# The even layer's order of chunks: the Fourier columns (context) and the context's output projection between the latent ranks' products and their use, and a tile of its own for `kvt`

## The chip, the cores and the metric

The kernel runs on one core of one Trainium2 chip. The metric is the device time of one execution in microseconds (us). Five engines work side by side and wait for each other by semaphores: TensorE (PE) does matrix products and transposes, VectorE (DVE), ScalarE (ACT) and GpSimd (POOL) do elementwise work, and SyncE (SP) issues the loads of the weights.

## The reference

Two blocks, one behind the other. The first has two layers (retention, dilated attention, gated MLP, and a feed-forward part). The second has an even and an odd layer, over 256 positions `x` and 256 positions of a context `ctx`. The change lies in the even layer alone:

```python
def mla_kv(kv_a, k_pe, kv_norm, w_kvb, rope):
    kv = (rmsnorm(kv_a, kv_norm) @ w_kvb).reshape(b, n, 8, 64 + 64)    # latent rank 256
    ...
def even_layer(h_lat, h_ctx, w_in, q_norm, w_qb, kv_norm, w_kvb, w_out, rope, ctx_out):
    f_in, f_gate, q_a, kv_a, k_pe, m_gate = split_cols(h_lat @ w_in, EVEN_SPLITS)
    cf_in, cf_gate, cq_a, ckv_a, ck_pe, cm_gate = split_cols(h_ctx @ w_in, EVEN_SPLITS)
    k_c, v_c = mla_kv(ckv_a, ck_pe, kv_norm, w_kvb, None)
    k_l, v_l = mla_kv(kv_a, k_pe, kv_norm, w_kvb, rope)
    q_l = mla_q(q_a, q_norm, w_qb, rope)                               # latent rank 384
    a_l = blocked_dense_attention(q_l, concat(k_c, k_l), concat(v_c, v_l), MLA_SCALE)
    y_l = concat([fourier_mix(f_in) * silu(f_gate), a_l * silu(m_gate)]) @ w_out
    q_c = mla_q(cq_a, q_norm, w_qb, None)
    a_c = dense_attention(q_c, k_c, v_c, MLA_SCALE)
    y_c = concat([fourier_mix(cf_in) * silu(cf_gate), a_c * silu(cm_gate)]) @ w_out
    return y_l, y_c
```

`h_lat` and `h_ctx` are the normed and modulated `x` and `ctx`. `fourier_mix` is the real part of a two-dimensional Fourier transform over positions and group columns.

## The kernel before, in words

Products in full accuracy: every float32 operand is split into a high and a low part, and each product is done as three products of the parts (`mm3`, `mmT`). Weights come from memory in pieces of up to 128x1024 (`raw`, three in flight in this layer), are split by ACT (`whi`) and by DVE or POOL in turn (`wlo`) into a ring of five, and a piece goes back to the ring when its last product is done. `plan` lists the pieces in the order of use, and SP's queue loads them in that order.

The even layer is one generator, `even_pass(b)`, run for `b = 0` (context) and `b = 1` (latents, the 256 positions of `x`). Each `yield` ends a step, and each step is one chunk of products over 256 positions:

- `kv`: 288 columns, the rank of keys and values with the rotary columns. Each tile of 128 positions is normed into `ka`, and a task transposes `ka`, splits it into `kvt` (`to_split`), and does the same for the rotary columns (`kp` into `kpT`).
- `qa`: 384 columns, the queries' rank, normed into `qa`, transposed and split by a task into `qtT`.
- `kvb`: keys `kT` and values `vs` from `kvt`. `qb`: queries `qT`, `qr` from `qtT`. After `qb` two tasks (`heads_task`) do the attention: four units of two heads for the context, eight for the latents, two at a time. The latents' eight are called four rounds here.
- `fi`: 512 columns; a task does the Fourier transform in four groups (`aa`, `yf`). `fg`, `mg`: gates of 512 columns each. `wo`: the output projection, two halves of 512 columns, eight blocks of the contraction each; blocks 0 to 3 need the Fourier part, 4 to 7 the attention.

When the context's `wo` is done, `modnorm_task` norms, transposes and modulates the context again (`crow`) for the odd layer.

TensorE's program is written in order at build time. A small planner (`Flow`) keeps an estimate of the time of each engine; after each `mm3` or `mmT`, `pump` lets up to three tasks whose due time has come write their next matmuls. Where a chunk needs a result (`F.wait`), the planner runs tasks until the result is due. So the tasks' matmuls stand between the products of whatever chunk is being written. The programs of ACT, DVE and POOL are ordered by the scheduler, by priorities; each of those engines takes its instructions in order.

In the kernel before, `kvt` is the tile `junk` (one buffer), which the norm of the latents at the end of the first block (`modnorm_task` with `junk`, events `eev[1]`) uses too. The `kv` tasks of both passes therefore yield until `eev[1]` of both tiles is set (lines 1744 and 1745).

Of the kernel before, what the change touches and what calls it, by code (L numbers as in the profile page):

```python
# [12 lines left out]
F32R = mybir.dt.float32r  # L13
BF16 = mybir.dt.bfloat16
I32 = mybir.dt.int32
AF = mybir.ActivationFunctionType
# [4 lines left out]
P = 128  # L21
# [98 lines left out]
LAT = 0.22  # L120
TR = "tr"
# [204 lines left out]
def block_kernel(ctx: ExitStack, tc: tile.TileContext, A, out, stop=None):  # L326
    nc = tc.nc
    pe = nc.tensor
    F = Flow()
    act, dve, gp = (Lane(F, n, e) for n, e in (("act", nc.scalar), ("dve", nc.vector), ("pool", nc.gpsimd)))  # L330
# [29 lines left out]
    def trtile(dt=F32):  # L360
        F.take_tr()
        return pt.tile([P, 512], dt, name="tr")
# [5 lines left out]
    def mm(o, lhsT, rhs, start, stop_, cost=None, **kw):  # L368
        n = 1
        for s in o.shape[1:]:  # L370
            n *= s
        pe.matmul(o, lhsT, rhs, start=start, stop=stop_, **kw)  # L372
        if cost is None:
            cost = max(0.107, n * 0.417e-3 + 0.003) if lhsT.dtype == F32R else 2 * max(0.107, n * 0.833e-3 + 0.003)
        F.now += cost
        F.chain = max(F.chain, F.now + LAT)
# [138 lines left out]
    def chunk_plan(b, key):  # L515
        if key == "kvb":
            for k in range(2):
                add(("e", b, key), A["e_w_kvb_2"][0], k, 1, [(0, D)])
        elif key == "qb":
            for k in range(3):  # L520
                add(("e", b, key), A["e_w_qb_2"][0], k, 1, [(0, 768)])
        elif key == "wo":
            for h in range(2):
                for k in range(0, 8, 2):
                    add(("e", b, "wo", h), eo, k, 2, [(h * 512, 512)])
        else:
            cc, n = {"kv": (1408, 288), "qa": (1024, 384), "fi": (0, 512), "fg": (512, 512), "mg": (1696, 512)}[key]
            add_chunk(("e", b, key), ew, cc, n, key in ("fg", "mg"))
    E_STEPS = ["kv", "qa", "kvb", "qb", "fi", "fg", "mg", "wo"]
    E_ORDER = [0] * 7 + [1] * 4 + [0] + [1] * 4  # L530
    at_step = [0, 0]
    for b in E_ORDER:
        chunk_plan(b, E_STEPS[at_step[b]])
        at_step[b] += 1
    ow, oo = A["o_w_in_2"][0], A["o_w_out_2"][0]
    for key, cc in (("kv", 1024), ("q0", 0), ("q1", 512), ("g0", 1536), ("g1", 2048)):
# [1041 lines left out]
    def work(name):  # L1578
        return w2.tile([P, 512], F32, name=name, tag="w")
# [11 lines left out]
    def etile(tag, shape, bufs=1, dt=F32, name=None):  # L1591
        return ep.tile([P] + shape, dt, name=name or tag, tag=tag, bufs=bufs)
# [11 lines left out]
    def chunk(key, n, toks, xs, evs, evac):  # L1604

        w = by_k(take(key, 4))
        for i, t in enumerate(toks):
            z = mmtile()
            for k in range(8):
                if k % 4 == 0:  # L1610
                    F.wait(evs[t][k // 4])
                mm3(z[:, :n], xs[t][0][:, k], xs[t][1][:, k], w[k], k == 0, k == 7)
                F.pump()
                if i == len(toks) - 1 and k % 2:
                    done()
            F.from_pe()
            evac(t, z)
# [86 lines left out]
    def even_pass(b):  # L1704
# [12 lines left out]

        def kvt_tile():
            if not box:
                box.append(jp.tile([P, 2, 2, 256], F32R, name="kvt", tag="junk"))  # L1720
            return box[0]

        def evac_kv(t, z):
            sq = small("ss")
            act.activation(dump(256), z[:, :256], AF.Square, scale=1.0 / 16.0, accum_out=sq)
            c = F.chain
            kp = etile("kp", [4, 32], 2)
            src = z[:, 256:288]
            if b == 1:
                kr = etile("kr", [64])  # L1730
                rotate(kr[:, :32].rearrange("p (h d) -> p h d", h=1), src.rearrange("p (h d) -> p h d", h=1),
                       axm[:, t * 64:(t + 1) * 64], 1, 16, kr[:, 32:64], dve)
                src = kr[:, :32]
            act.activation(kp, src[:, None, :].to_broadcast([P, 4, 32]), AF.Copy)
            F.chain, c = c, F.chain
            r = power(sq, "rkv", 1.0, EPS)
            ka = work("ka")
            F.chain = max(c, F.chain)
            act.activation(ka[:, :256], z[:, :256], AF.Copy, scale=r)
            F.free_mm()  # L1740

            def task():
                yield
                yield eev[1][0][1]
                yield eev[1][1][1]
                yield TR
                tr = trtile()
                for j in range(2):
                    transpose(tr[:, j * P:(j + 1) * P], ka[:, j * P:(j + 1) * P], ident)
                tc_ = slice(t * P, (t + 1) * P)  # L1750
                kvt = kvt_tile()
                to_split(tr, [col("e_kv_norm_2", j) for j in range(2)], kvt[:, 0, :, tc_], kvt[:, 1, :, tc_])
                F.free_tr()
                F.set(kv_ev[t])
                yield TR
                tr = trtile()
                transpose(tr[:, :P], kp.rearrange("p a f -> p (a f)"), ident)
                n0 = (2 * b + t) * P
                F.from_pe()
                halves(kpT[:, 0, n0:n0 + P], kpT[:, 1, n0:n0 + P], tr[:, :P])  # L1760
                F.free_tr()
                F.set(kp_ev[t])
            F.spawn(task())
# [39 lines left out]
            F.spawn(task())  # L1803
        chunk(("e", b, "qa"), 384, range(2), xs, evs, evac_qa)
        yield

        n0 = 2 * b * P
        w = by_k(take(("e", b, "kvb"), 2))
# [155 lines left out]
            F.spawn(heads_task(par))  # L1964
        yield

        def evac_fi(t, z):
            us[t] = etile("g2", [512], 4, name="us")
            act.activation(us[t], z, AF.Copy)
            F.free_mm()  # L1970
            F.set(u_ev[t])
        chunk(("e", b, "fi"), 512, range(2), xs, evs, evac_fi)
        yf = etile("yf", [4, 256])

        def fourier_task():
            yield u_ev[0]
            yield u_ev[1]
            for g in range(4):
                yield TR
                tr = trtile()  # L1980
                for a in range(2):
                    mm(tr[:, :258], us[a][:, g * P:(g + 1) * P], dft[:, a * 258:(a + 1) * 258], a == 0, a == 1)
                t3 = tr[:, :258].rearrange("p (s n) -> p s n", s=2)
                aa = work("aa").rearrange("p (s n) -> p s n", s=2)
                act.activation(aa[:, :, 0:128], t3[:, :, 0:128], AF.Copy)
                F.chain -= LAT
                act.activation(aa[:, 0, 128:256], t3[:, 0, 128:0:-1], AF.Copy)
                F.chain -= LAT
                act.activation(aa[:, 1, 128:256], t3[:, 1, 128:0:-1], AF.Copy, scale=-1.0)
                F.free_tr()  # L1990
                yield TR
                tr = trtile()
                mm(tr[:, :256], cds[:, 0:P], aa[:, 0], True, False)
                mm(tr[:, :256], cds[:, P:2 * P], aa[:, 1], False, True)
                act.activation(yf[:, g], tr[:, :256], AF.Copy)
                F.free_tr()
            F.set(yf_ev)
        F.spawn(fourier_task())
        yield

        sgf, sgm = [None, None], [None, None]

# [7 lines left out]
        def product_task():  # L2010
            yield yf_ev
            for i in range(2):
                yield gf_ev[i]
                dst = yf[:, 2 * i:2 * i + 2].rearrange("p k n -> p (k n)")
                gp.tensor_tensor(dst, dst, sgf[i], op=OP.mult)
                F.set(yg_ev[i])
        yg_ev = [Ev(), Ev()]
# [12 lines left out]
        def split_task():  # L2030
            for i in range(2):
                yield yg_ev[i]
                v = yf[:, 2 * i:2 * i + 2]
                act.activation(XH[b][:, 2 * i:2 * i + 2], v, AF.Copy)
                dve.tensor_tensor(XL[b][:, 2 * i:2 * i + 2], v, XH[b][:, 2 * i:2 * i + 2].bitcast(F32), op=OP.subtract)
                for k in (2 * i, 2 * i + 1):
                    F.set(yT_ev[k])
            for i in range(2):
                yield gm_ev[i]
                for h in range(4 * i, 4 * i + 4):  # L2040
                    yield at_ev[h]
                v = at_box[0][:, 2 * i:2 * i + 2]
                vf_ = v.rearrange("p k n -> p (k n)")
                dve.tensor_tensor(vf_, vf_, sgm[i], op=OP.mult)
                k0 = 4 + 2 * i
                act.activation(XH[b][:, k0:k0 + 2], v, AF.Copy)
                dve.tensor_tensor(XL[b][:, k0:k0 + 2], v, XH[b][:, k0:k0 + 2].bitcast(F32), op=OP.subtract)
                for k in (k0, k0 + 1):
                    F.set(yT_ev[k])
            F.set(split_ev[b])  # L2050
# [289 lines left out]
```

## Time and profile before

| | |
|---|---|
| time, median of three runs | 1141.86 us (1140.38 to 1144.85) |
| time of the profiled execution | 1140.57 us |
| its span, first to last instruction | 1138.8 us |
| busy: PE, DVE, ACT, POOL | 95%, 58%, 51%, 19% of the span |
| the even layer in the span | 699.5 to 968.0 us |

The span is what the trace covers; the 1.8 us between it and the execution's time lie outside the trace. A matmul's end is modelled, so consecutive matmuls overlap in the rows, and a busy share of 100% does not say that TensorE can go no faster. A row's idle time is the time in which an engine had nothing running, and the name beside it is the instruction that ended it.

### The profile page before, as it was taken

To read this page: it belongs to the slowest core of one execution; us is meant where nothing else is said; L and a number is where in the kernel's file an instruction comes from. 1 tells how busy PE (TensorE), PEld (TensorE's weight loads), DVE (VectorE), ACT (ScalarE), POOL (GpSimd) and SP (SyncE) were. 2 spreads that over 40 slices of the span, in tenths; PEclk is the share of its full clock that TensorE was granted. 3 is DMA by queue.
4 is the path that set the end of the run, shared out by engine and by line. 5 is a ranking of instruction groups with operands and counts; after the bars stand their busy time and mean duration, and the time that the engine had idled before them with its cause. 6 is when DMAs were issued, how large, how long until landed. Compare 5 with 4: busy or idle time off the path is not lost. (4 is left out here: it accounts for less than half of the span.)

```text
span 1138.8 us, 18328 instructions
## 1 busy us (share of the span) xinstructions
PE 1076.7 (95%) x7066; PEld 924.2 (81%) x7066; DVE 658.0 (58%) x1233; ACT 580.1 (51%) x1080; POOL 215.7 (19%) x170
## 2 busy tenths in 40 slices
PE   6999999999999999989999998899999999998996
PEld 5899778999987889768999887788877687777865
DVE  6776676555556677658655555542655425664563
ACT  5554564434335555446344344655656554555762
POOL 5221100000001120200000002431453124351120
PEclk8999999999999999999999999899999999999998
DMA  8654468566763745567756642641453324343210
GB/s 268 211 181 149 160 207 277 188 219 207 224 227 105 241 154 162 172 216 260 236 173 199 216 124 81 196 145 48 128 190 97 110 76 153 130 153 106 90 30 30
DMA packets 115991, 186.20 MB, mean 164 GB/s; under 512 B 6939, under 2 KB 84104, under 8 KB 115904
## 3 DMA queue, kind: packets, MB, share of 16 engines
q1 hardware_dynamic: 112896, 179.33, 48.9%
q10 hardware_dynamic: 2512, 5.44, 1.5%
q8 instruction: 55, 0.90, 0.3%
q0 software_dynamic: 496, 0.27, 0.1%
q14 instruction: 32, 0.26, 0.1%
HBM read 183.95 MB, written 1.06 MB: 162 GB/s over the span
## 5 line engine op out<-in xcount | busy, mean ns | idle before, releaser
L280 DVE TENSOR_TENSOR wlo<-raw,whi 128x1024 fp32r<-128x1024 f32 (+4 forms) x260 | 316.6, 1223 | 195.8 <-ACT whi L280 191.9
L280 ACT ACTIVATE whi<-raw 128x1024 fp32r<-128x1024 f32 (+4 forms) x313 | 301.9, 975 | 224.9 <-PE mm L372 134.0
L372 PE MATMUL mm<-xh,whi 128*128 128x256 f32 x768 | 225.3, 293 | 0.5 <-DVE fh L280 0.5
L372 PE MATMUL mm<-whi,xh 128*128 128x384 f32 (+2 forms) x564 | 218.4, 387 | 6.4 <-ACT whi L280 2.8
L372 PE MATMUL mm<-xh,wlo 128*128 128x256 f32 x768 | 217.4, 283 | 0.0
L372 PE MATMUL mm<-xl,whi 128*128 128x256 f32 x768 | 217.4, 283 | 0.0
L372 PE MATMUL mm<-wlo,xh 128*128 128x384 f32 (+2 forms) x564 | 208.3, 369 | 6.0 <-POOL wlo L280 3.5
L372 PE MATMUL mm<-whi,xl 128*128 128x384 f32 (+2 forms) x564 | 207.3, 368 | 1.3 <-DVE xl L280 1.3
L280 POOL TENSOR_TENSOR wlo<-raw,whi 128x1024 fp32r<-128x1024 f32 (+4 forms) x53 | 110.9, 2094 | 335.8 <-ACT whi L280 279.9
L372 PEld LDWEIGHTS mm<-xh,whi 128*128 128x128 f32 x768 | 147.3, 192 | 8.4 <-issue 7.3
L372 PEld LDWEIGHTS mm<-xh,wlo 128*128 128x128 f32 x768 | 147.6, 192 | 0.9
L372 PEld LDWEIGHTS mm<-xl,whi 128*128 128x128 f32 x768 | 147.3, 192 | 0.0
L372 PEld LDWEIGHTS mm<-whi,xh 128*128 128x128 f32 x564 | 109.2, 194 | 26.1 <-issue 6.0
L372 PEld LDWEIGHTS mm<-wlo,xh 128*128 128x128 f32 x564 | 109.4, 194 | 17.4 <-POOL wlo L280 4.5
L372 PEld LDWEIGHTS mm<-whi,xl 128*128 128x128 f32 x564 | 109.1, 193 | 13.6 <-DVE xl L280 2.1
L372 PE MATMUL sc<-whi,fhs 128*128 128x512 f32 x352 | 114.7, 398 | 0.0
L372 PEld LDWEIGHTS sc<-whi,fhs 128*128 128x128 f32 x352 | 66.1, 188 | 18.0 <-issue 2.1
L372 PE MATMUL sc<-wlo,fhs 128*128 128x512 f32 x176 | 69.6, 395 | 0.0
L280 POOL TENSOR_TENSOR rpost<-pe,mhalf 128x1 f32<-128x1 f32 x8 | 4.3, 542 | 255.5 <-DVE pe L280 255.5
L280 ACT ACTIVATE pp<-tr 128x512 f32<-128x512 f32 x56 | 32.7, 594 | 23.1 <-PE tr L379 22.8
L372 PE MATMUL tr<-rawm,mlh 128*32 128x256 f32 x384 | 41.0, 384 | 0.0
L372 PEld LDWEIGHTS sc<-wlo,fhs 128*128 128x128 f32 x176 | 33.1, 188 | 7.0
(342 smaller groups left out, 1393.7 us busy)
## 6 DMA issues: line engine op xcount, KB each, us to landing
raw<-in_w_gate_up_dram SPq DMA_DIRECT2D x72, 512.0 KB, 4.1
rawm<-in_w_mod_dram SPq DMA_DIRECT2D x48, 512.0 KB, 6.2
raw<-in_w_down_dram SPq DMA_DIRECT2D x44, 512.0 KB, 4.1
raw<-in_w_in_dram SPq DMA_DIRECT2D x56, 384.0 KB, 3.7
raw<-in_e_w_in_dram SPq DMA_DIRECT2D x24, 512.0 KB, 3.9
raw<-in_o_w_in_dram SPq DMA_DIRECT2D x20, 512.0 KB, 3.6
raw<-in_w_out_dram SPq DMA_DIRECT2D x16, 512.0 KB, 4.5
raw<-in_w_gate_up_dram SPq DMA_DIRECT2D x32, 256.0 KB, 4.1
```

The lines of the kernel that those rows point to most:

```text
L280: return fn(*args, **kw)
L372: pe.matmul(o, lhsT, rhs, start=start, stop=stop_, **kw)
```

## The change

The context's `fi` chunk moves from behind `qb` to between `qa` and `kvb`. The context's `wo` moves from behind the latents' `qb` to between the latents' `qa` and `kvb`. The latents' own steps keep their order. `kvt` gets a tile of its own in the layer's pool, and the two yields on `eev[1]` go. The list of weight pieces (and so of loads) follows the steps.

```
steps before: c.kv c.qa c.kvb c.qb c.fi c.fg c.mg  l.kv l.qa l.kvb l.qb  c.wo  l.fi l.fg l.mg l.wo
steps after:  c.kv c.qa c.fi c.kvb c.qb c.fg c.mg  l.kv l.qa  c.wo  l.kvb l.qb l.fi l.fg l.mg l.wo
```

```diff
-    E_STEPS = ["kv", "qa", "kvb", "qb", "fi", "fg", "mg", "wo"]
-    E_ORDER = [0] * 7 + [1] * 4 + [0] + [1] * 4
+    E_STEPS = [["kv", "qa", "fi", "kvb", "qb", "fg", "mg", "wo"], ["kv", "qa", "kvb", "qb", "fi", "fg", "mg", "wo"]]
+    E_ORDER = [0] * 7 + [1] * 2 + [0] + [1] * 6
...
-        chunk_plan(b, E_STEPS[at_step[b]])
+        chunk_plan(b, E_STEPS[b][at_step[b]])
...
-                box.append(jp.tile([P, 2, 2, 256], F32R, name="kvt", tag="junk"))
+                box.append(etile("kvt", [2, 2, 256], dt=F32R))
...
-                yield eev[1][0][1]
-                yield eev[1][1][1]
                 yield TR
...
         chunk(("e", b, "qa"), 384, range(2), xs, evs, evac_qa)
         yield
+
+        ybox_e = [None]
+
+        def fi():
+            def evac_fi(t, z):
...
+            chunk(("e", b, "fi"), 512, range(2), xs, evs, evac_fi)
+            yf = ybox_e[0] = etile("yf", [4, 256])
+
+            def fourier_task():
...
+            F.spawn(fourier_task())
+        if b == 0:
+            fi()
+            yield
...
             F.spawn(heads_task(par))
         yield
...
+        if b == 1:
+            fi()
+            yield
```

The bodies of `evac_fi` and `fourier_task` are the same as before, and the gates read `ybox_e[0]` in place of `yf`.

## Rows read from the trace of the kernel before

**Rows 1.** The page, part 1: busy time and share of the span.
```profile
PE 1076.7 (95%) x7066; PEld 924.2 (81%) x7066; DVE 658.0 (58%) x1233; ACT 580.1 (51%) x1080; POOL 215.7 (19%) x170
```

**Rows 2.** Windows by stage: length, engines' busy time, granted clock, DMA share, GB/s.
```profile
core 0: us, PE busy (x) PEld busy (x) DVE busy (x) ACT busy (x) POOL busy (x), PEclk, DMA share, GB/s
699.50:729.30 29.80, 22.26 (x113) 20.07 (x112) 17.95 (x39) 17.55 (x42) 12.42 (x11) 0.83 0.53 164
805.10:838.70 33.60, 29.72 (x201) 27.40 (x200) 21.57 (x45) 21.92 (x52) 16.02 (x13) 1.00 0.51 169
851.80:928.40 76.60, 75.05 (x534) 55.52 (x533) 34.09 (x64) 44.72 (x95) 21.19 (x12) 1.00 0.32 97
```

**Rows 3.** Waits of PE, 690 to 970 us: total, times, longest.
```profile
PE tr L379 <- ACT qa L280: 4.1, 3, 2.5
PE mm L372 <- ACT xh L280: 2.0, 1, 2.0
...
PE s L372 <- ACT pp L280: 1.6, 1, 1.6
PE mm L372 <- POOL wlo L280: 1.4, 1, 1.4
PE tr L379 <- DVE qtT L280: 1.2, 1, 1.2
```

**Rows 4.** Windows inside the context's `qa`, columns as in rows 2.
```profile
713.20:718.50 5.30, 5.27 (x20) 5.18 (x20) 1.28 (x3) 1.71 (x4) 1.39 (x2) 0.50 0.87 257
718.50:726.60 8.10, 4.45 (x25) 3.85 (x23) 5.46 (x16) 5.39 (x13) 5.11 (x4) 0.92 0.53 165
726.60:729.30 2.70, 2.62 (x9) 2.53 (x10) 2.37 (x8) 1.37 (x5) 0.14 (x1) 0.50 0.85 266
```

**Rows 5.** Timeline of PE at the end of the context's `qa`.
```profile
724.18 0.55 PE L379 MATMUL tr<-c,qa 128*128 128x128 f32 x3 [2.52 <-ACT qa L280]
...
724.74 0.33 PE L372 MATMUL mm<-wlo,xh 128*128 128x384 f32 x1
724.91 0.34 PE L372 MATMUL mm<-whi,xl 128*128 128x384 f32 x1
...
726.68 0.69 PE L379 MATMUL tr<-c,ka 128*128 128x128 f32 x2 [1.21 <-DVE qtT L280]
...
729.30 0.34 PE L372 MATMUL mm<-kvt,whi 128*128 128x256 f32 x1
```

**Rows 6.** Windows of PE for tile `mm` alone: length, busy, matmuls, clock, DMA.
```profile
742.70:751.40 8.70, 8.51 (x38) 1.00 0.60 179
751.40:773.70 22.30, 11.07 (x64) 1.00 0.38 114
773.70:797.10 23.40, 11.25 (x76) 1.00 0.13 39
838.70:851.80 13.10, 12.91 (x56) 1.00 0.50 159
851.80:867.80 16.00, 8.49 (x31) 1.00 0.40 117
867.80:889.30 21.50, 11.27 (x40) 1.00 0.38 111
889.30:907.50 18.20, 10.37 (x49) 1.00 0.40 116
907.50:928.40 20.90, 8.18 (x50) 1.00 0.14 52
928.40:942.70 14.30, 14.27 (x118) 1.00 0.34 112
```

**Rows 7.** Timeline at 883 to 886 us: ACT, then PE.
```profile
883.51 1.15 ACT L280 ACTIVATE crow<-crow,rmod 128x1024 f32<-128x1024 f32 x1 [3.03 <-POOL rmod L280]
...
885.20 0.66 PE L372 MATMUL s<-pp,vs 128*64 128x128 f32 x8 [1.55 <-ACT pp L280]
```

**Rows 8.** Groups of DVE by form, 699 to 970 us: busy, mean ns, idle before.
```profile
L280 DVE TENSOR_SCALAR crow<-tr,modA,modT 128x128 f32<-128x128 f32 x16 | 5.6, 403 | 0.2 <-PE tr L379 0.2
```

More of the change, by code (lines that the diff above doesn't have):

```diff
@@ L1805, in even_pass @@
         yield
+        ybox_e = [None]
+        def fi():
+            def evac_fi(t, z):
+                us[t] = etile("g2", [512], 4, name="us")
+                act.activation(us[t], z, AF.Copy)
+                F.free_mm()
+                F.set(u_ev[t])
+            chunk(("e", b, "fi"), 512, range(2), xs, evs, evac_fi)
+            yf = ybox_e[0] = etile("yf", [4, 256])
+            def fourier_task():
+                yield u_ev[0]
+                yield u_ev[1]
+                for g in range(4):
+                    yield TR
+                    tr = trtile()
+                    for a in range(2):
+                        mm(tr[:, :258], us[a][:, g * P:(g + 1) * P], dft[:, a * 258:(a + 1) * 258], a == 0, a == 1)
+                    t3 = tr[:, :258].rearrange("p (s n) -> p s n", s=2)
+                    aa = work("aa").rearrange("p (s n) -> p s n", s=2)
+                    act.activation(aa[:, :, 0:128], t3[:, :, 0:128], AF.Copy)
+                    F.chain -= LAT
+                    act.activation(aa[:, 0, 128:256], t3[:, 0, 128:0:-1], AF.Copy)
+                    F.chain -= LAT
+                    act.activation(aa[:, 1, 128:256], t3[:, 1, 128:0:-1], AF.Copy, scale=-1.0)
+                    F.free_tr()
+                    yield TR
+                    tr = trtile()
+                    mm(tr[:, :256], cds[:, 0:P], aa[:, 0], True, False)
+                    mm(tr[:, :256], cds[:, P:2 * P], aa[:, 1], False, True)
+                    act.activation(yf[:, g], tr[:, :256], AF.Copy)
+                    F.free_tr()
+                F.set(yf_ev)
+            F.spawn(fourier_task())
+        if b == 0:
+            fi()
+            yield
         n0 = 2 * b * P
@@ L1965, in even_pass @@
         yield
[L1967 to L1999, printed above, removed]
+        if b == 1:
+            fi()
+            yield
         sgf, sgm = [None, None], [None, None]
@@ L2013, in product_task @@
                 yield gf_ev[i]
-                dst = yf[:, 2 * i:2 * i + 2].rearrange("p k n -> p (k n)")
+                dst = ybox_e[0][:, 2 * i:2 * i + 2].rearrange("p k n -> p (k n)")
                 gp.tensor_tensor(dst, dst, sgf[i], op=OP.mult)
@@ L2032, in split_task @@
                 yield yg_ev[i]
-                v = yf[:, 2 * i:2 * i + 2]
+                v = ybox_e[0][:, 2 * i:2 * i + 2]
                 act.activation(XH[b][:, 2 * i:2 * i + 2], v, AF.Copy)
```

## Prediction

> **What bounds the kernel now.** I read the page first: TensorE is busy for 95% of the span and no other engine for more than 58% [rows 1], so its program sets the time, and a change of order, which removes no product, can only remove or add time in which TensorE stands still or runs at its lower clock. Next the windows by stage: the context's first chunks (699.5 to 729.3) have 22.26 us of PE in 29.8 at a mean granted clock of 0.83; the latents' `kv` to `qb` lose 33.60 - 29.72 = 3.9 us; the stage of the latents' heads (851.8 to 928.4) loses 1.55 us of 76.6 [rows 2]. Then the waits, to see what ends each idle stretch: inside the layer they are single events, the longest 2.5, 2.0, 1.6, 1.4 and 1.2 us [rows 3]. So what is to be had is the idle time and slow clock ahead of 729.3, which the change touches in part; what is at risk is the cover of the heads, which the change takes from.
>
> **The early part.** Removed are the two yields on `eev[1]` and the shared buffer; added is 4 KB per partition, no instruction. The transposes of `ka` and `kp` (six matmuls of 128 columns) are now due when `ka` is, that is in the end of `kv` or the start of `qa`; before they stood at the end of `qa`. There TensorE waited first 2.52 us for ACT `qa`, then ran a few products, then waited 1.21 us for DVE `qtT`, which held a transpose buffer [rows 5]. From 726.6 to 729.3 it ran at a granted clock of 0.50, the 1.2 GHz level [rows 4]. `kvb` began at 729.30 [rows 5].
>
> After the change the 2.52 us wait stays: the norm of `qa`'s first tile comes from the same instructions behind the same latents' norm. Behind its three transposes nine products of `qa` are left in the timeline, the third at 724.91, 0.17 us behind the second [rows 5], so the last of them is through at 724.91 + 7 x 0.17 = 726.1, and `fi` starts there in place of `kvb` at 729.30: a gain of 3.2 us. Where the moved transposes land TensorE has waits of its own already (1.4 us for POOL `wlo` among them [rows 3]), which cover them; if they don't, six transposes cost their own time, at most 1.1 us by the 0.55 us of three [rows 5]. If the slow clock of the last 2.7 us comes anyway, behind the 2.52 us of idle time, half of 2.7 is lost again: 3.2 - 1.35 = 1.85. I take the middle, **-2.5**. The ends: 0 (the wait for ACT `qa` only grows by what was saved) and -3.2 - 2.5 - 2.65 = -8.4 (that wait goes too, and the first slow stretch, 5.3 us at 0.50 [rows 4], runs at full clock).
>
> The clock's rows: 0.50 at 713.2 to 718.5 after a stretch with waits, 0.92 in the next window, 0.50 again at 726.6 after two more waits [rows 4, 5]. The Trainium skill (TensorE: Matmul & The Clock Gate, part 1, "What's actually happening") says that the low clock is the default state and that activity releases it; these rows agree. By that rule every stretch of idle time which the change moves elsewhere carries a slow stretch with it, and the sum would be worse by what is said under the third rival; the sum here does not hold it.
>
> **Context's fi and heads.** `fi` is 48 products of 512 columns, 8.51 / 38 = 0.22 us each, 11 us in all [rows 6]; it moves with its four groups of Fourier matmuls and costs nothing by itself. But it was cover for the context's heads. From the end of `qb` to their start the products of the chunk took 8.5 us, and in the heads 11.07 + 11.25 [rows 6]: 30.8 asked. Left behind `qb` are `fg` and `mg`, 192 products of 256 columns at 14.3 / 118 = 0.121 us [rows 6], 23.3 us, and then the latents' `kv` and `qa`, 48 x 0.17 = 8.2 for `qa` [rows 5] and 288/384 of it, 6.1, for `kv`: 37.6 before the context's `wo` needs the heads. That covers 30.8, so nothing is added; if 10% more were asked, 33.9 is still covered. On the other side `kvt` and `qtT` are ready long before `kvb`.
>
> **Context's wo ahead of the latents' kvb.** It gives the transposes and splits of `ka` and `qa` 21 us (96 x 0.22). Of the waits for ACT `qa` two are left, 4.1 - 2.5 = 1.6 us in all [rows 3]; the one of the second tile falls behind the first `kvb` products and is now covered. I take a quarter of the sum, **-0.4**, ends 0 and -1.6.
>
> The context's second norm now falls into the latents' `kvb` and `qb`, before it fell into the heads. There ACT stood 3.03 us behind it (its `crow` waited for POOL `rmod`), `pp` was queued behind it on ACT, and TensorE waited 1.55 us for `pp` [rows 7, 3]. That wait goes: **-1.5** (ends 0 and -1.55). In its new place the same ACT instruction can stand ahead of `kT`, `vs` and `qT`, and DVE has 16 pieces of 0.4 us [rows 8] ahead of their low parts. TensorE has six output buffers for these chunks, so it stops only if more are late. I put **+1.0**, between nothing and the 3.03 us of that ACT wait.
>
> **The latents' heads.** This is the price of the move. `wo` was the cover of the time between `qb` and the first unit (12.9 us of products) and of the first rounds; the four rounds asked 8.49 + 11.27 + 10.37 + 8.18 = 38.3 us of products, and 14.3 us of `mg` were left over behind them [rows 6]. After the change `fi` (11 us) takes the place of the 12.9 ahead of the first unit, 1.9 short. `fg` and `mg` give 23.3, and the latents' `wo` can begin with blocks 0 to 5 on its first tile, 18 products of 512 columns at 0.22, 4.0 us. So 38.3 + 1.9 - 23.3 - 4.0 = 12.9 us are asked and not there. They are missing at the end, in the last one and a third of the four rounds (38.3 / 4 = 9.6 each). What they cost depends on what they were: where a product was written because no task was due yet, it becomes idle time; where a task was due and merely waited its turn behind products, the rounds close up. The trace shows no round without cover. Bounds: all of it close-up, 0 added, and all of it idle, 12.9 less the 2.0 us for ACT `xh` that stand at this place already [rows 3], +10.9. In a round of 16.0 to 21.5 us two units alternate [rows 6], so when one waits the other mostly has something to write; I take 40% as idle, 5.2 - 2.0 = **+3.2**.
>
> **Loads and queues.** The number, size and order within a chunk of the loads on SP's queue are the same. `fi` ahead of `kvb` and `wo` ahead of the second `kvb` put chunks with 0.22 us per product between the narrow ones, so a piece has more time to arrive and be split; I cost this at nothing, and if a piece is late it costs what late pieces cost now, 1.4 us [rows 3].
>
> **Sum.** -2.5 - 0.4 - 1.5 + 1.0 + 3.2 = -0.2, against the profiled execution's own 1140.57 (span 1138.8 and 1.8 us around it): 1140.4, which I give as 1140. The profiled execution lies 1.3 us below the median of 1141.86, and inside the runs shown. A change of less than 0.5% of that, 5.7 us, I call no change.
>
> **Rivals.**
> - *Cancel (the forecast)*: the early gain and the lost cover are of one size. For it: both are read from rows and both are a few us. 1137 to 1146, likeliest 1140; chance 0.51.
> - *The early gain without the loss*: the rounds close up (+0 in place of +3.2), and the start runs at full clock through its first slow stretch (a further 2.65): 1140.57 - 2.5 - 2.65 - 0.4 - 1.5 + 1.0 + 0 = 1134.5. For it: the one wait above a microsecond that ended ahead of that stretch is 1.4 us, for POOL `wlo` [rows 3]. Against: those waits are for weights and `ka`, which the change does not bring forward. Chance 0.27.
> - *The heads end after mg*: nearly all of the 12.9 us become idle time. It decides from 9 us added on, 1140.57 - 3.4 + 9.0 = 1146.2; all of it gives 1140.57 - 3.4 + 10.9 = 1148.1, and 1150.7 with one slow stretch like the first (5.3 us at half clock, 2.65 lost [rows 4]). For it: `pump` writes a task as soon as it is due, so the products between tasks were mostly waits by the planner's reckoning. Against: two units share the round. Chance 0.16.
> - *The context's norm blocks kvb and qb*: ACT and DVE stand ahead of each evacuation, 3.0 us each in `kvb` and in `qb`, and the first unit later by as much: 1140.57 - 2.5 - 0.4 - 1.5 + 3.2 + 9.0 = 1148.4. Against: six output buffers. Chance 0.06.
>
> Together: faster 0.27, same 0.51, slower 0.22. The range leaves out the ends of the early gain below -8 and a stalled tail with more than one slow stretch: 1132 to 1150; for the forecast alone 1137 to 1146.
>
> **What would show it.** Right: the waits of PE lose DVE `qtT` 1.2 and the single ACT `pp` 1.6; the first product of `fi` comes 2 to 3 us earlier than 729.3; the window of the latents' `kvb` and `qb` shows waits of about a microsecond; between the end of `mg` and the middle of the latents' `wo` PE is idle for 4 to 6 us, waiting for ACT `pe`, `pp` or `xh`. Wrong: that idle time is missing, or is above 10 us; the clock at 713 to 719 is 1.00; or the latents' `kv` and `qa` wait for the context's heads.

## The result and the profile after

The changed kernel takes 1150.38 us (median of six runs, 1146.89 to 1153.77) against 1141.80 for six runs of the kernel before: 1.0068 times the time, 95% interval 1.0048 to 1.0088. That is 8.6 us slower: the interval lies clear of 1, and the difference is above the 5.7 us (0.5%) below which the prediction speaks of no change. The profiled execution has 1153.77 us and a span of 1152.0. Of its 13.2 us above the profiled execution of before, 2.0 lie ahead of the even layer (its first product comes at 701.47, before at 699.51) and 2.9 behind it, in code that the change doesn't touch. Both shift from run to run: over the fourteen profiles of this study the start lies between 696.8 and 702.8, the part behind the layer takes 170.9 to 174.0, and neither goes with the order. So below I compare lengths of stages inside the layer, taken from PE's timeline, never points of time.

The page, part 1, has the same counts as [rows 1]; PE has 5.0 us more of busy time for the same 7066 matmuls:

```profile
PE 1081.7 (94%) x7066; PEld 932.6 (81%) x7066; DVE 658.3 (57%) x1233; ACT 580.3 (50%) x1080; POOL 214.9 (19%) x170
```

The stages of the layer, in us. A stage begins with the first matmul of its step; the ends of `qb` and of `mg` are the ends of their last matmuls. "Whole" runs from the context's first `kv` product to the first transposes of the next norm behind the latents' `wo`.

| stage | before | after | difference |
|---|---|---|---|
| context's `kv` to latents' `kv` | 105.61 | 103.04 | -2.57 |
| latents' `kvb` and `qb` | 6.56 + 8.68 | 6.48 + 20.77 | +12.01 |
| the rest from latents' `kv` to the end of `mg`, the context's `wo` in it | 122.44 | 122.08 | -0.36 |
| end of `mg` to the next norm | 24.86 | 24.16 | -0.70 |
| whole | 268.15 | 276.53 | +8.38 |

In this pair of profiles the layer is 8.4 us longer, against 8.6 us between the medians, and one line carries it: the latents' `kvb` and `qb`. The windows of after show that stage and the heads; columns as in [rows 2]:

```profile
846.08:873.30 27.22, 16.89 (x108) 15.75 (x107) 18.00 (x34) 14.05 (x25) 9.80 (x9) 0.82 0.38 121
887.20:953.84 66.64, 65.64 (x540) 52.52 (x540) 22.44 (x43) 37.30 (x86) 12.04 (x6) 1.00 0.24 73
```

The same two steps before:

```profile
823.60:838.83 15.23, 13.25 (x95) 12.04 (x95) 8.17 (x16) 9.05 (x19) 6.32 (x6) 1.00 0.60 200
```

PE is idle there for 27.22 - 16.89 = 10.3 us, before for 2.0, and it ran at a granted clock of 0.82, before at 1.00. DVE is the engine with the most work of the stage now, 18.0 us against 8.2. What ends the idle time is in PE's waits, 690 to 990 us, which answer to [rows 3]:

```profile
PE s L372 <- DVE pe L280: 6.6, 1, 6.6
PE mm L372 <- DVE rt L280: 3.6, 1, 3.6
PE tr L379 <- ACT qa L280: 3.6, 2, 1.9
PE mm L372 <- ACT whi L280: 2.0, 1, 2.0
PE tr L379 <- ACT ka L280: 1.8, 1, 1.8
...
PE mm L372 <- ACT xh L280: 1.3, 1, 1.3
PE s L372 <- ACT pp L280: 1.0, 1, 1.0
```

The first two waits, which the kernel before hardly has (`rt` 0.9, the other not at all), make 10.2 us. The first is put down to `pe`, a sum of the norm that no product reads. The view of the waits of the weight loads, 803 to 955 us, gives the same wait another name:

```profile
PEld s L372 <- DVE wlo L280: 6.8, 1, 6.8
```

PE's timeline shows what stood at that place. the `s<-qtT,wlo` that waits is the first product of `qb` that uses the low part of the third weight piece:

```profile
853.14 0.79 PE L372 MATMUL s<-qtT,whi 128*128 128x256 f32 x2
860.51 0.58 PE L372 MATMUL s<-qtT,wlo 128*128 128x256 f32 x1 [6.58 <-DVE pe L280]
...
867.15 0.27 PE L372 MATMUL mm<-whi,qtT 128*128 128x256 f32 x1
871.05 0.58 PE L372 MATMUL mm<-whi,qtT 128*128 128x256 f32 x1 [3.62 <-DVE rt L280]
```

And this is what DVE did in that time. `crow` and `xl<-crow` are the context's norm; `wlo<-raw,whi 128x512` at 859.78 is the low part that PE awaits (`pe` at 860.38, behind it, is only the last instruction before the product started):

```profile
850.77 2.00 DVE L280 TENSOR_SCALAR crow<-tr,modA,modT 128x128 f32<-128x128 f32 x6
854.84 0.69 DVE L280 TENSOR_TENSOR xl<-crow,xh 128x512 fp32r<-128x512 f32 x1 [2.06 <-ACT xh L280]
855.45 0.72 DVE L280 TENSOR_SCALAR crow<-tr,modA,modT 128x128 f32<-128x128 f32 x2
856.09 0.68 DVE L280 TENSOR_TENSOR kT<-s,kT 128x512 fp32r<-128x512 f32 x1
856.68 0.41 DVE L280 TENSOR_TENSOR wlo<-raw,whi 128x256 fp32r<-128x256 f32 x1
857.22 2.65 DVE L280 TENSOR_TENSOR xl<-crow,xh 128x512 fp32r<-128x512 f32 x1
859.78 0.68 DVE L280 TENSOR_TENSOR wlo<-raw,whi 128x512 fp32r<-128x512 f32 x1
860.38 0.14 DVE L280 TENSOR_SCALAR pe<-ss 128x1 f32<-128x1 f32 x1
...
865.62 2.01 DVE L280 TENSOR_SCALAR crow<-tr,modA,modT 128x128 f32<-128x128 f32 x6 [1.03 <-PE tr L379]
867.74 0.69 DVE L280 TENSOR_TENSOR xl<-crow,xh 128x512 fp32r<-128x512 f32 x1
868.35 0.72 DVE L280 TENSOR_SCALAR crow<-tr,modA,modT 128x128 f32<-128x128 f32 x2
868.99 0.68 DVE L280 TENSOR_TENSOR qT<-mm,qT 128x512 fp32r<-128x512 f32 x1
869.59 0.41 DVE L280 TENSOR_TENSOR qpe<-mm,dft 128x256 f32<-128x256 f32 x1
869.92 0.68 DVE L280 TENSOR_TENSOR xl<-crow,xh 128x512 fp32r<-128x512 f32 x1
870.52 0.48 DVE L280 TENSOR_TENSOR rt<-mm,dft 128x128 f32<-128x128 f32 x2
```

The high part of the same piece was ready by 853.80, in ACT's timeline:

```profile
852.88 0.92 ACT L280 ACTIVATE whi<-raw 128x512 fp32r<-128x512 f32 x2
```

So an instruction of 0.68 us started 6.0 us after its data were there: DVE stood waiting for the norm's `xh` (until 854.84), then did an `xl`, two `crow` and another `xl` of the norm, and between them a key's evacuation and the narrow part of the same piece; the last `xl` took 2.65 us where its like takes 0.69. The second wait is the second tile's norm, at 865.62 to 870.6, ahead of the evacuation of the rotary queries (`rt`). The kernel writes the rotary queries of both tiles into the two halves of one output tile (one `ztile()` ahead of the loop), and PE began the second half at 871.05, when the first half's `rt` ended (871.00): a larger number of output buffers would not have spared it this wait.

Each wait has a slow stretch behind it. Windows of after:

```profile
853.90:860.50 6.60, 0.03 (x1) 0.00 (x0) 5.55 (x9) 4.39 (x7) 2.51 (x1) 0.70 0.25 92
860.50:867.40 6.90, 6.88 (x46) 6.71 (x46) 3.63 (x9) 2.67 (x4) 1.46 (x1) 0.79 0.70 230
867.40:871.05 3.65, 0.03 (x1) 0.00 (x1) 3.48 (x9) 0.94 (x2) 0.00 (x0) 0.89 0.00 0
871.05:876.00 4.95, 4.95 (x16) 4.37 (x17) 2.62 (x4) 2.95 (x3) 3.44 (x3) 0.50 0.01 2
876.00:880.00 4.00, 4.00 (x17) 3.18 (x17) 0.75 (x1) 0.00 (x0) 3.70 (x2) 0.87 0.80 240
```

In the three stretches where PE worked the clock takes 6.9 x 0.21 + 4.95 x 0.50 + 4.0 x 0.13 = 4.4 us. With 8.3 us more of idle time that is 12.7, of which 12.0 show in `kvb` and `qb` and 0.9 between the end of `qb` and the first unit of the heads (12.99 to 13.85).

What else the prediction named: the waits for `qtT` (1.2) and the 1.6 for `pp` are gone from the list, a `pp` of 1.0 remains. The context's `qa` ends with one wait for ACT `qa` of 1.9 in place of 2.5, and `fi` begins at 729.14, 27.67 us after the first `kv` product; `kvb` began 29.79 us after it before [rows 5]:

```profile
726.56 0.65 PE L379 MATMUL tr<-c,qa 128*128 128x128 f32 x3 [1.89 <-ACT qa L280]
...
729.14 0.63 PE L372 MATMUL mm<-whi,xh 128*128 128x512 f32 x1
```

The heads, which were to be short of cover, are not. Windows for tile `mm` alone from the first unit to the last matmul of the heads, after (columns: length, PE busy, matmuls, clock, DMA, GB/s):

```profile
887.18:952.93 65.75, 29.97 (x182) 1.00 0.24 75
```

They take 65.75 us with 29.97 us of products between; before they took 75.54 with 37.7 (both are busy times, with each product's modelled end).

### The profile page after: what moved, and what is told of

Same layout as the page of the kernel before. It is cut to its first block, busy times and chain, and to the rows that moved or that the text cites. A ratio compares the mean times of both kernels' runs of the same rounds, so it can differ in the third digit from the quotient of the medians.

```text
span 1152.0 us, 18317 instructions
## 1 busy us (share of the span) xinstructions
PE 1081.7 (94%) x7066; PEld 932.6 (81%) x7066; DVE 658.3 (57%) x1233; ACT 580.3 (50%) x1080; POOL 214.9 (19%) x170
## 5 line engine op out<-in xcount | busy, mean ns | idle before, releaser
L280 DVE TENSOR_TENSOR wlo<-raw,whi 128x1024 fp32r<-128x1024 f32 (+3 forms) x260 | 313.4, 1210 | 205.9 <-ACT whi L280 198.1
```

The source lines that it names most:

```text
L280: return fn(*args, **kw)
```

## The experiments

The theory after this reading: the context's norm, which follows the context's `wo`, now falls into `kvb` and `qb`, and stands on DVE ahead of the low part of a weight piece. Rivals: the kernel loses by the lack of cover or by the order itself and the norm only shows it (the wait would then move elsewhere); the separate `kvt` tile or the context's `fi` is at fault; the low part is late for its place in the ring or on its engine, whatever stands ahead of it. Each of the twelve kernels was timed against the kernel before on the same chip; e5 to e8 ran on another chip than the rest, so between those groups ratios are compared, not times. Stages in the text are those of the table above.

**The change in its parts.** Four kernels: the two moves each alone, the tile alone, and the full order with the norm held back until the latents' queries are through.

e1, the context's `fi` and the tile, `wo` where it was:
```diff
-    E_ORDER = [0] * 7 + [1] * 2 + [0] + [1] * 6
+    E_ORDER = [0] * 7 + [1] * 4 + [0] + [1] * 4
```


> kvt's tile and the context's fi ahead of kvb; wo stays behind the latents' qb. The collision theory expects 1139 (the 2.6 us gained up to the end of the context's mg, and none of the loss), no wait over 2 us in the latents' qb. A rival (the heads of the context, shifted by fi, run into the latents' chunks and cause the late waits) expects 1145 or more.

e2, `wo` and the tile, `fi` where it was (both rows of `E_STEPS` as before):


> kvt's tile and the context's wo ahead of the latents' kvb; fi stays behind qb. The collision theory expects 1151 to 1153: the 11.6 us that the changed kernel lost between the latents' kv and the end of their mg, less about 1 us from the tile, with waits of 3 to 7 us in the latents' qb and a granted clock near 0.5 behind them. If both moves are needed for the loss, 1142 to 1145.

e4, the tile alone (e1 and e2 together):


> The order of before; only kvt has its own tile and the two yields on eev[1] are gone. The theory (collision: the context's second norm, moved into the latents' kvb and qb, blocks DVE there and nothing else costs much) expects 1140.5, about 1 us under before, because the wait for DVE qtT (1.2 us) ahead of kvb goes and one for the kv rank comes in part. A rival (the early gain is the tile's, not the order's) expects all of the 2.6 us that the changed kernel gained up to the end of the context's mg: 1139.2.

e3, after, with the norm held:
```diff
+    def held(task):
+        yield hold_ev
+        yield from task
...
             F.set(qr_ev)
+            if b == 1:
+                F.set(hold_ev)
...
-                        F.spawn(modnorm_task(lambda t=t: crow[:, t], 1, 1, place(t), oev[0][t]))
+                        F.spawn(held(modnorm_task(lambda t=t: crow[:, t], 1, 1, place(t), oev[0][t])))
```


> The changed kernel, but the context's second norm is not begun before the latents' queries are transposed (it waits for an event set behind the split of qr), so it lies among the latents' heads as in the kernel before. The collision theory expects 1137 to 1139: the two waits in qb (6.6 and 3.6 us) fall below 1 us each, the slow clock behind them goes, the early gain stays. Rival one (the latents' heads and qb lack the cover of wo) expects 1147 or more, since the order of the products is unchanged. Rival two (the weight pieces of kvb and qb are split late behind those of wo) expects the 6.6 us wait to stay: 1145 to 1148.

| kernel | us | to before (95%) | context part | `kvb` + `qb` | heads |
|---|---|---|---|---|---|
| e1 `fi` | 1140.75 | 0.9987 (0.9973 to 1.0001) | 103.32 | 15.23 | 75.52 |
| e2 `wo` | 1150.85 | 1.0075 (1.0058 to 1.0092) | 104.94 | 27.55 | 65.76 |
| e4 tile | 1143.63 | 1.0006 (0.9991 to 1.0022) | 105.06 | 16.00 | 75.53 |
| e3 norm held | 1144.95 | 1.0021 (1.0009 to 1.0034) | 102.99 | 17.33 | 71.93 |

e2 has the whole loss and e1 none of it, so the move of `wo` is at fault. e1 keeps the early gain (-2.3 us), the tile alone has 0.55 of it. That part of the layer takes 105.6 to 106.9 us in the three profiles of the old order without the tile (before, e6, e12) and 102.1 to 104.0 in the nine with `fi` moved, so the gain of `fi` stands clear of the scatter and that of the tile does not. e3 takes the first wait away and with it two thirds of the loss. Not all: in the same stage waits for `rt` and `vs` are left, and in the heads new ones for `aa` and `crow`, here PE's waits of e3, 800 to 970 us:

```profile
PE mm L372 <- DVE rt L280: 2.5, 1, 2.5
...
PE tr L379 <- ACT aa L280: 1.6, 2, 1.1
PE mm L372 <- ACT vs L280: 1.5, 1, 1.5
PE tr L372 <- DVE crow L280: 1.0, 1, 1.0
```

The hold acts on the order in which the program is written. The scheduler, which orders ACT by priorities, still put the norm's square early. ACT's timeline of e3 has the second tile's square, 1.04 us long, and its scaling (`crow`) among the evacuations of keys and values:

```profile
852.06 1.04 ACT L280 ACTIVATE dump<-crow 128x1024 bf16<-128x1024 f32 x1
...
853.10 0.57 ACT L280 ACTIVATE kT<-s 128x512 fp32r<-128x512 f32 x1
853.58 0.58 ACT L280 ACTIVATE vs<-mm 128x512 f32<-128x512 f32 x1
854.06 1.15 ACT L280 ACTIVATE crow<-crow,rmod 128x1024 f32<-128x1024 f32 x1
```

And where the norm's transposes come in the heads they stand between the latents' Fourier steps (`aa`). So e3 does not separate the order from the norm; the next pair does.

**Without the norm, and with its competitor on another engine.** In e5 (after) and e6 (before) the context's norm is left out:
```diff
-                        F.spawn(modnorm_task(lambda t=t: crow[:, t], 1, 1, place(t), oev[0][t]))
+                        [F.set(e) for e in oev[0][t]]
```


> The changed kernel without the context's second norm (its squares, scaling, 16 transposes, modulation and split are left out; the odd layer takes what lies in the context's operands). To be read against e6_no_norm_before. The collision theory expects it 2 to 4 us under e6: no wait above 1.5 us in the latents' qb, the early gain of 2.6 us kept. The cover theory (taking wo from behind qb costs by itself, and holding the norm in e3 left 2.8 us over before for that reason) expects 2 to 4 us over e6.

> The kernel before without the context's second norm, the partner of e5_no_norm_after. About 4 us under before: 2.3 us of transposes and the 1.55 us wait for ACT pp behind the norm: 1137 to 1139.

e8 leaves the norm as it is and sends the low parts of the three pieces of the latents' `qb` to POOL, which takes them in turn with DVE otherwise. In the changed kernel DVE has two of the three, each in two instructions (128x512 and 128x256), so e8 moves four instructions. e11 sends all three pieces to DVE. e12 is e8's edit in the kernel before.
```diff
     def pool_lo(key, i):
+        if key == ("e", 1, "qb"):
+            return True
```


> The changed kernel, but the low parts of the three weight pieces of the latents' qb are all worked out on POOL (before: pieces in turn on POOL and DVE). If the 6.6 us wait is for the DVE piece that stands behind the norm in DVE's order, it falls below 2 us and the clock behind it stays up: 1145 to 1147, with the 3.6 us wait for DVE rt still there or moved. If the wait is for an evacuation by DVE (the output buffer), it stays: 1149 to 1151.

> The changed kernel with the low parts of all three pieces of the latents' qb on DVE, the opposite of e8_qb_pool. If pieces behind the norm in DVE's order make the loss, it stays or grows: 1150 to 1154, a wait of 6 to 9 us in qb. If any regrouping of these pieces helps, as a matter of the scheduler's luck, 1142 to 1146.

> The kernel before with the edit of e8_qb_pool alone. There no norm stands beside qb, so the collision theory expects no change: 1141 to 1143. If the edit is good by itself (POOL has time that DVE lacks), 1138 to 1140, and e8 says little on the cause.

| kernel | us | to before (95%) | `kvb` + `qb` | heads | whole layer |
|---|---|---|---|---|---|
| e5 after, no norm | 1135.82 | 0.9935 (0.9917 to 0.9953) | 13.97 | 65.76 | 262.77 |
| e6 before, no norm | 1138.61 | 0.9955 (0.9939 to 0.9971) | 15.25 | 66.47 | 266.82 |
| e8 after, low parts on POOL | 1141.91 | 0.9988 (0.9974 to 1.0002) | 18.72 | 65.75 | 268.71 |
| e11 after, low parts on DVE | 1148.95 | 1.0046 (1.0028 to 1.0063) | 27.57 | 65.75 | 275.71 |
| e12 before, low parts on POOL | 1144.08 | 1.0009 (0.9990 to 1.0027) | 16.38 | 75.53 | 270.94 |

Without the norm the new order is the faster one, 1135.8 (1133.5 to 1137.2) against 1138.6 (1135.3 to 1141.0), and `kvb` and `qb` take less than in the kernel before, 13.97 us. That settles it against the order itself and against the lack of cover. e8 changes nothing but the engine of four instructions, and the 6.6 us wait goes; the granted clock is 1.00 over its whole `kvb` and `qb`. DVE's and POOL's timelines of e8 at the place:

```profile
852.77 0.69 DVE L280 TENSOR_TENSOR xl<-crow,xh 128x512 fp32r<-128x512 f32 x1 [4.10 <-ACT xh L280]
853.38 0.72 DVE L280 TENSOR_SCALAR crow<-tr,modA,modT 128x128 f32<-128x128 f32 x2
...
854.81 2.39 DVE L280 TENSOR_TENSOR xl<-crow,xh 128x512 fp32r<-128x512 f32 x1
```
```profile
851.57 2.50 POOL L280 TENSOR_TENSOR wlo<-raw,whi 128x512 fp32r<-128x512 f32 x2 [1.14 <-issue]
```

DVE waits for `xh` here too (4.10 us), now with no weight piece of `qb` behind it, and POOL makes the two low parts of one piece in the meantime; the 128x512 takes it 1.27 us against DVE's 0.68. What is left in e8's stage are 2.6 us for `rt` (the second wait, which the edit doesn't touch), 1.0 for POOL `wlo` and 0.7 for ACT `whi`. e11 keeps the loss, with 3.6 us for `rt` as in the changed kernel, and here PE's waits name the low part themselves:

```profile
PE s L372 <- DVE wlo L280: 5.5, 1, 5.5
```

In e11 the low part stands behind less of the norm (it starts 2.6 us after PE stopped, at 855.54) but takes 2.85 us itself, beside a POOL `wlo` of 2.72; of the 5.5 us, some 2.2 are of that kind. e12 is level with the kernel before, so POOL is no better place as such: it helps only where DVE's program is stopped.

**Later places for the norm.** e7 holds it until the latents' `mg`, with a scale of its square made from `mg`'s result, so that no scheduler can bring it forward. e9 does the same from the first output tile of the latents' `wo`, with a pause in the written order between the two tiles and ahead of the transposes. The first edit is in both, the second is e9's.
```diff
-        act.activation(dump(n), src, AF.Square, scale=1.0 / math.sqrt(n), accum_out=s)
+        act.activation(dump(n), src, AF.Square, scale=late[0] if late else 1.0 / math.sqrt(n), accum_out=s)
...
+                if b == 1 and h == 0 and t == 0:
+                    late.append(small("late", bufs=1))
+                    dve.tensor_scalar(late[0], tmp[:, 0:1], 0.0, 1.0 / 32.0, op0=OP.mult, op1=OP.add)
+                    F.set(hold_ev)
```


> The changed kernel with the context's second norm begun only when the first half of the latents' mg gate is there, held by its data (the scale of its squares is a column worked out from that gate, with the same value of 1/32), so that no engine can take it earlier; it lies in the latents' wo. The collision theory expects 1137 to 1140: kvb, qb and the heads are free of it, and wo has DVE and ACT idle for about half its length. The cover theory expects 1143 or more, from idle time in the heads. A third outcome: the norm is late for the odd layer's first chunk, 2 to 5 us ahead of it.

> The changed kernel with the context's second norm held by its data until the latents' first output tile is there, its transposes written 2.5 us behind the planner's end of the scaling and the second tile 2 us later, so that nothing of it stands among the latents' products of keys and queries or their heads. The collision theory expects 1138 to 1140 with before at 1142: e5's time plus the 2.3 us of transposes plus about a microsecond. If the norm is too late for the odd layer's first chunk, waits for DVE crow or ACT xh of 2 to 6 us appear there: 1142 to 1146.

e7: 1144.92 us, 1.0024 (1.0008 to 1.0039). `kvb` and `qb` take 14.04, but the planner reckoned the norm ready too early and had its transposes written among the last units: PE waits three times for DVE `crow`, 5.3 us in all, with the units behind them, and the heads take 76.52. e9: 1141.20, 0.9984 (0.9967 to 1.0000). From the latents' `kv` to the end of `mg` it takes 134.77, as e5 does without the norm (134.65). In `wo` the norm costs again: 32.0 us from the end of `mg` to the next norm against 24.2. Of the 7.8 us between, 2.7 are waits for low parts (2.0 for DVE, 0.7 for POOL), 1.8 the norm's own 16 transposes, and about 2 are nine products of the next chunk that PE did in that time; the rest was not taken apart. PE's waits of e9, 800 to 970 us:

```profile
PE mm L372 <- DVE wlo L280: 2.0, 1, 2.0
```

**Is there any cover to spare?** e10 is e5 with the latents' `fi` moved ahead of their `kvb` too, so that 11 us more of products are gone from behind `qb` (the norm is left out).
```diff
-    E_STEPS = [["kv", "qa", "fi", "kvb", "qb", "fg", "mg", "wo"], ["kv", "qa", "kvb", "qb", "fi", "fg", "mg", "wo"]]
+    E_STEPS = [["kv", "qa", "fi", "kvb", "qb", "fg", "mg", "wo"], ["kv", "qa", "fi", "kvb", "qb", "fg", "mg", "wo"]]
```


> e5_no_norm_after (no second norm of the context) with the latents' fi also moved ahead of their kvb, so that 11 us more of cover go from behind qb. The prediction's price for missing cover (40% of what is asked and not there) expects 4 to 5 us over e5. If the heads close up by themselves and only the norm had stretched them, 0 to 2 us over e5.

1144.24 us, 1.0005 (0.9992 to 1.0018); by the ratios that is 8.0 us more than e5, and the layer takes 269.79 against 262.77. Now the heads do end behind `mg`, some 28 us behind it, and the waits that the prediction looked for are there, 800 to 970 us:

```profile
PE tr L379 <- ACT pe L280: 3.2, 4, 1.4
PE mm L372 <- ACT xh L280: 2.1, 1, 2.1
```

So the cover has an end; the change under study doesn't reach it (its heads end 0.9 us ahead of `mg`).

Against what was expected of them, e3, e7 and e9 came out 6, 5 and 1 us above the upper end that the collision theory gave, because the norm costs in each new place too; e8 came out 3 us and e11 1 us below the lower end; e4, e1 and e12 came out 3, 2 and 1 us above theirs; and e10's 7.0 us in the layer are well above the 4 to 5 by the prediction's price.

## Why the prediction was wrong

Its sum was -0.2 us, the layer shows +8.4. Step by step:

- **The early part: the size right, the way only in part.** -2.5 was taken, -2.57 measured (e1: -2.3). The wait for `qtT` went, as it said. But the moved transposes were not covered: one of `ka` waits 1.8 us of its own, and products wait 2.0 for ACT `whi` where they waited 0.8, while the 1.4 for POOL `wlo` is gone. The end of `qa` still runs slow, its last products 0.32 us apart in place of 0.17. That these come to the middle of the sum is in part luck. The two ends didn't come: the wait for ACT `qa` shrank from 2.5 to 1.9 and neither grew nor went, and the first slow stretch stayed (0.66 at 710 to 720 us).
- **`kvt`'s own tile.** With the yields gone and nothing else it gives 0.55 us (e4), no more than the scatter; the gain is that of `fi` ahead of `kvb` (e1).
- **The context's norm in `kvb` and `qb`: the step that failed.** It was put at +1.0, between nothing and the 3.03 us of ACT's wait [rows 7], and measured +12.0. The argument was that TensorE has six output buffers and stops only if more are late. That counts one way in which DVE and ACT can hold PE, the evacuation of results, and leaves out the other: PE's next operand. A weight piece's low part goes through DVE's program in order, and stood behind DVE's wait for the norm's `xh`, two `xl` and two `crow` (e8, which moves only the low parts of two pieces, takes `qb` from 20.77 to 12.22). The number of buffers did not bear on the evacuation that did stop PE either: `rt` holds up the second half of the same buffer. The bound of 3.03 was too low for two reasons that the rows before already held: the norm has two tiles, and the clock falls behind each stop (4.4 us here). Of the 16 pieces of 0.4 us on DVE [rows 8], 6.4 us in all, the prediction spoke and then didn't price them.
- **The wait for `pp` behind the norm (-1.5), the context's `wo` as cover (-0.4) and the latents' heads (+3.2): +1.3 together, -0.36 measured.** The list of waits gives `pp` 1.0 in place of 1.6. The term mis-sized is the heads. Of the two ends that were given, all close-up and all idle, it was all close-up: 65.75 us at a granted clock of 1.00, with a wait of 1.3 for ACT `xh` at their end where 2.0 stood before. The 4 to 6 us of idle time behind `mg` are missing, which the prediction named as a sign of being wrong. The 12.9 us "asked and not there" came out too large for two reasons. The first is that two measures are mixed. The 38.3 us of the four rounds [rows 6] are busy time, in which a product that stands among the units' matmuls counts with its whole modelled length (0.27 to 0.50 us); `fi`, `fg` and `mg` are counted from start to start, at 0.22 and 0.121 us. The window of the heads of after shows what that makes: its 182 products of 256 columns are 22.0 us from start to start and 29.97 of busy time. The same stretch of before (851.8 to 928.4, by tile `mm`) holds 91 products of 512 columns and 75 of 256; one of three groups of each:

```profile
L372 PE MATMUL mm<-whi,xl x31: 388/397/398, 851.5 to 898.3; 128*128 128x512 f32 x31
...
L372 PE MATMUL mm<-xl,whi x25: 274/281/288, 899.2 to 927.6; 128*128 128x256 f32 x25
```

  From start to start that is 20.0 + 9.1 = 29.1 us, so 29.1 + 1.9 - 23.3 - 4.0 = 3.7 were missing, not 12.9, and 40% of that less the 2.0 for `xh` puts the term at about nothing. The second reason is that the 38.3 had the norm's own delays in them: the kernel before without its norm has heads of 66.47 us in place of 75.54, and asks, in the window for tile `mm` of e6 (busy time again),

```profile
849.96:916.43 66.47, 33.60 (x136) 1.00 0.36 102
```

  33.6, before 37.7 over the same stretch. A demand read off a stretch holds every delay of the stretch.
- **Loads and queues at nothing: no load is named in the new waits, but the low part of a piece is.** The sentence "a piece has more time to arrive and be split" was right for the loads; the splitting's place in DVE's queue was not looked at.

Of the rivals it was the last, the norm blocking `kvb` and `qb`, given 0.06 and 1148.4 us; its place was right, its mechanism half: the stop in `rt` is an evacuation, as it said (3.6 us), the larger one an operand. What would have shown it ahead of time is a list of DVE's instructions in the order in which the scheduler would have put them behind `wo`: six `crow`, `xl`, two `crow`, `xl` per tile, and between them the low parts of `qb`'s pieces. The first output of `qb` needs all three pieces at once: its first product started at 852.56, and after seven of them PE stopped for the third piece.

The rule on the clock that the prediction held beside its sum (the Trainium skill, TensorE: Matmul & The Clock Gate, part 1, "What's actually happening") is that the low clock is the default and activity releases it. This trace agrees: 0.50 from 871.05 to 876.00, straight behind an idle stretch of 3.6 us, and the 4.4 us that the three slow stretches cost were in no term.

Why one `xl<-crow` took 2.65 us and not 0.69: it ran from 857.22 to 859.87, and POOL had a `wlo` of 2.51 us from 856.79 to 859.30. The Trainium skill (SBUF — State Buffer, "Who interferes with whom") has a rule for that: a DVE instruction with two inputs in SBUF contends with a GpSimd instruction that reads SBUF, over a shared pair of ports that it calls an exclusive lock, and issue order decides which of the two blocks. The times fit, as do e8's 2.39 us beside a POOL `wlo` of 2.40 and e11's 2.85 beside 2.72; no run here takes the POOL instruction away to prove it. By these rows it is 2 of the 6.6 us. The POOL row:

```profile
856.79 2.51 POOL L280 TENSOR_TENSOR wlo<-raw,whi 128x1024 fp32r<-128x1024 f32 x1 [5.00 <-ACT whi L280]
```

What stays open: e9, e1 and e8 come out at 0.9984 to 0.9988 of the kernel before, which is inside what can be told from no change. A version with the new order's 2.8 us (e5 against e6) and the norm at no cost was not found.

## What to carry to other kernels

Before a step is moved, write down the elementwise work that follows it, and for each engine of that work what the in-order program will have behind it in the new place; not results to be evacuated alone, but the operands of the next products. A small instruction that makes an operand can cost the whole of what stands ahead of it, that work's own waits included, and the slow clock after. Products that are set against each other have to be counted in one measure: from start to start, not as the busy time of one tile among others. A hold in the order in which a program is written doesn't hold an engine that a scheduler orders: it takes a dependence on data, or another engine.

## What the runs showed that I had not expected

The wait for one DVE instruction of 0.68 us cost 6.6 us, and the releaser that the list of waits names (`pe`) is not the one awaited; the view of the weight loads names it. The heads of eight units close up by 9 us when the elementwise work of another step leaves them (75.54 to 66.47), though PE was 98% busy there before, and in the same two profiles the layer as a whole is only 1.3 us shorter (268.15 to 266.82): the products that filled the gap were no saving, only work brought forward.
